# Three token mixers dealt over a projection stream: another order of the mixers' inputs and of emission

## The chip, the cores and the metric

The kernel runs on one core of a Trainium2 chip. The metric is the device time of one execution in microseconds (us); shown is the median of several runs. One execution is also profiled. Engines are named PE (matrix), DVE (vector), ACT (scalar), POOL (GpSimd) and SP (sync); PEld is PE's weight load.

## The reference

Two layers of a decoder trunk on 256 tokens of width 1024, in float32. In each layer:

```python
x = LN(a*x + 0.5*SwiGLU_1(x))                       # width 2816
h = x @ w_in                                        # split among three mixers and merge gates
x = LN(a*x + (sum_b sigmoid(h_gate_b) * (Mixer_b(h_b) @ w_branch_b)) @ w_o)
x = LN(a*x + 0.5*SwiGLU_2(x))
x = LN(a*x + sigmoid(x @ w_pg) * (p[i] @ w_pp))
```

The mixers are causal and independent of each other: branch 0 is RWKV-7 (8 heads of 64), branch 1 is gated linear attention, GLA (4 heads, keys 64, values 128), branch 2 is Gated DeltaNet (4 heads of 128, a convolution over 4 tokens ahead of it). RWKV and DeltaNet both need the inverse of a unit triangular matrix for each chunk. Each mixer is a chain: small products on PE, each followed by work on ACT or DVE that the next product waits for.

## The kernel before

All weights come from memory as blocks of 128 x 1024 (`raw`). ACT rounds a block to a short format (`hi`), DVE subtracts (`lo`), and each product of activations with weights is three matmuls (high with high, high with low, low with high) of 256 or 512 columns. The feed-forward parts (`h`, `y`, `tb`) run as a steady stream of such matmuls. Four `raw` and four `hi`/`lo` buffers turn over, loaded by SP in the order in which `plan()` lists the blocks.

The mixer part of a layer has four generators:

- S, `stream`: the columns of `w_in`, one block of 256 columns at a time (PE writes `cb`), in the order of `MIX`. First come two fixed blocks (`wa`; `misc`, which has the small inputs of all three mixers, and `ab`, DeltaNet's gates). Then the items of `MIX`: `C_R`, `C_K`, `C_V` are RWKV's inputs (tile `c`, one shift step on DVE per 128 columns), `C_DQ`, `C_DK`, `C_DV` DeltaNet's (tile `c`, a convolution of three DVE steps per 128 columns), `C_LQ` GLA's queries and keys (`lqk`), `C_LV` its values (`st`). A pair such as `(2, 0)` is half of the merge gate of branch 2: `cb` is copied to `sg` and sent to memory (`gd`) until it is needed (`sgate`). `("w", b, h)` is the product of the finished branch b with half h of `w_branch` (`pj`), into the merge `mg`.
- R, `rwkv`: `pw`; normed keys (`kk`, `sq`); operands spread to `ls` and `bk`; grams (PE `gram`, DVE masks into `gram` and `ls`, ACT copies); transposes `bkt`; the inverse (`rig`, `rigt`, `riab` on DVE, then `rix`, `rih`, `ric`); `vm`, `bon`; four chunks (`rp`, `ru`, `ry`, `rd`), and per half of the tokens an output (`rv`, `pg`, `ro`).
- D, `gdn`: gates (`x`, `gcol`, `grow`, `dd`), norms (`un`), `pk`, `pq`, its inverse (`gig` to `gih`), `gtt` to `gto`, `ktr`, two chunks (`gv`, `gd`, `go`).
- L, `gla`: `gk`, a scan (`lxb`), seven levels (DVE and ACT make `lw`, PE `lg`, DVE writes `latt` under a mask), `lc`, `lo`.

D's first step makes `x` from `ab` in some 20 small steps on DVE with an exponential on ACT between them, and its second step starts with `gcol` and `grow`.

`mixers` steps through the letters of `ORDER`; a letter advances its generator to its next bare `yield`. A generator that yields a name waits for an input, and then the stream (or the maker of that name) is stepped until it is there:

```python
def step(self, name):
    for need in self.threads[name]:
        if need is None:
            return
        while need not in self.got:
            self.step(self.maker.get(need, "S"))
    self.over.add(name)
```

So code is emitted in this order. The build then sets each engine's queue from it with a list scheduler of its own, which may move instructions that are not pinned to program order. On the chip every engine takes its queue in order: an instruction that waits holds all behind it.

`plan()` and `merge` follow `MIX` as well: the last item's half decides which half of `w_o` comes last.

Of the kernel before, what the change touches and what calls it, by code (L numbers as in the profile page):

```python
# [44 lines left out]
C_R, C_K, C_V, C_WA, C_GLO = 0, 512, 1024, 1536, 1664  # L45
C_LQ, C_LK, C_LV, C_LGK, C_LG = 1824, 2080, 2336, 2848, 2864
C_DQ, C_DK, C_DV, C_DAB, C_DG = 3376, 3888, 4400, 4912, 4920
# [4 lines left out]
B_LG, B_DG, B_ALOG, B_DT, NB = 0, 128, 256, 260, 264  # L52
K_ID, K_ONES64, K_M0, K_M1, K_M16, K_OFF16, K_INCL, K_HP, K_HF, K_CENT, NK = (
    0, 128, 256, 384, 512, 544, 672, 800, 802, 804, 932)
MIX = (C_R, C_K, C_DK, C_LV, (0, 0), C_V, C_LQ, (0, 1), C_DQ, (2, 0), (1, 1), C_DV, (2, 1), (1, 0), ("w", 0, 0),
       ("w", 1, 1), ("w", 0, 1), ("w", 1, 0), ("w", 2, 0), ("w", 2, 1))
ORDER = ("RRSRSSSDSSRSRRSSSRRRRRRRRRRSSRSRRRSDRRRRRSRSRDRRRRRRRRDRDSDRLDRRDRDLRDDSDSSSLDLDRLRDRRRDRDDRRRDLRLDD"
         "SDDDDSDLLSDDDLLRDLSDLLRRLLDSSDSDSLLSSSSDSLDS")
LEVELS = (64, 32, 16, 8, 4, 2, 1)


# [5 lines left out]
def plan():  # L67
# [13 lines left out]
    for i in range(DEPTH):  # L81
# [4 lines left out]
        out.append(("fmisc", i))  # L86
        for item in MIX:
            if isinstance(item, tuple) and item[0] == "w":
# [5 lines left out]
            else:  # L94
                out.extend(("fcol", i, item + 256 * u) for u in range(2))
        last = MIX[-1][2]
        out.extend(("wo", i, h, u) for u in (1 - last, last) for h in range(2))
# [137 lines left out]
class Trunk:  # L235
# [434 lines left out]
    def mixers(self, i):  # L670
# [3 lines left out]
        self.threads = {"S": self.stream(i), "R": self.rwkv(i), "D": self.gdn(i), "L": self.gla(i)}  # L674
        for name in ORDER + "RDLS":
            self.step(name)
# [4 lines left out]
    def stream(self, i):  # L681
# [26 lines left out]
        yield  # L708
        for item in MIX:
            if isinstance(item, tuple) and item[0] == "w":  # L710
                yield "b%d" % item[1]
                self.project(i, *item[1:])
                if item != MIX[-1]:
                    yield
# [949 lines left out]
```

## Time and profile before

| what | us |
|---|---|
| median of 3 runs (1572.3 to 1577.93) | 1574.76 |
| the profiled execution, its own time | 1568.71 |
| span of its instructions | 1566.9 |
| PE busy | 1494.9 (95%) |
| PEld busy | 1356.7 (87%) |
| DVE busy | 1058.5 (68%) |
| ACT busy | 873.3 (56%) |
| mean granted clock of PE | 0.981 |

The mixer parts run from about 227 to 545 us and from about 1007 to 1325 us of the span. A busy PE is not PE at its peak, since matmuls overlap in the records. Matmul groups in float32 without the split appear twice as often in the trace as in the program's queue.

### The profile page before, as it was taken

What the parts mean: (1) busy time and instruction counts of PE and PEld (TensorE: products, weight loads), DVE (VectorE), ACT (ScalarE), POOL (GpSimd) and SP (SyncE); (2) the same over time, 40 slices, a digit from 0 to 9 for tenths busy, and PEclk for the clock granted to TensorE, in tenths of its full rate; (3) what the DMA queues carried; (4) which work ended last, traced back from release to release, by engine and by line L of the source; (5) the groups of instructions that cost most, each with busy time, mean ns of one, the idle gap of its engine ahead of it and who ended that gap; (6) DMA issues with size and microseconds to landing.
All of it is one profiled execution on the core that took longest, in us unless ns stands there. A gap on an engine that the chain in (4) does not pass through costs nothing. (4 is left out here: it accounts for less than half of the span.)

```text
span 1566.9 us, 27601 instructions
## 1 busy us (share of the span) xinstructions
PE 1494.9 (95%) x11280; PEld 1356.7 (87%) x11280; DVE 1058.5 (68%) x1597; ACT 873.3 (56%) x1229; POOL 49.1 (3%) x85
## 2 busy tenths in 40 slices
PE   8999999988998999999999999998989889999997
PEld 7999889887987989998789997897979879899986
DVE  5555757787975875556865557577789658745567
ACT  5544558856654554445654445587665555644453
POOL 0000000000002000000000000000000020000001
PEclk9999999989999999999999999999999999999999
DMA  7765655532424655656555666554425256656562
GB/s 257 264 215 189 216 190 161 169 127 80 151 84 168 233 184 177 223 189 216 177 180 192 216 189 194 195 170 153 136 75 156 82 200 219 188 170 222 189 217 81
DMA packets 79775, 277.96 MB, mean 177 GB/s; under 512 B 9376, under 2 KB 9760, under 8 KB 79648
## 3 DMA queue, kind: packets, MB, share of 16 engines
q1 hardware_dynamic: 75744, 262.76, 51.8%
q0 software_dynamic: 3616, 13.11, 2.2%
q8 instruction: 88, 1.44, 0.4%
q10 hardware_dynamic: 288, 0.33, 0.1%
q14 instruction: 39, 0.32, 0.1%
HBM read 264.63 MB, written 11.53 MB: 176 GB/s over the span
## 5 line engine op out<-in xcount | busy, mean ns | idle before, releaser
L223 DVE TENSOR_TENSOR lo<-raw,hi 128x1024 fp32r<-128x1024 f32 (+1 forms) x459 | 555.4, 1220 | 316.1 <-ACT hi L223 313.7
L223 ACT CAST hi<-raw 128x1024 fp32r<-128x1024 f32 (+1 forms) x459 | 474.9, 1047 | 430.1 <-PE h L223 144.1
L223 PE MATMUL h<-xh,hi 128*128 128x256 f32 x1088 | 306.2, 282 | 5.9 <-ACT hi L223 5.5
L223 PE MATMUL h<-xl,hi 128*128 128x256 f32 x1088 | 305.8, 281 | 0.8 <-DVE xl L223 0.8
L223 PE MATMUL h<-xh,lo 128*128 128x256 f32 x1088 | 305.4, 281 | 0.0
L223 PE MATMUL cb<-xh,hi 128*128 128x256 f32 x864 | 247.1, 286 | 14.4 <-DVE c L223 11.1
L223 PE MATMUL cb<-xl,hi 128*128 128x256 f32 x864 | 244.5, 283 | 0.0
L223 PE MATMUL cb<-xh,lo 128*128 128x256 f32 x864 | 243.4, 282 | 0.0
L223 PEld LDWEIGHTS h<-xh,hi 128*128 128x128 f32 x1088 | 204.9, 189 | 7.3 <-ACT hi L223 5.5
L223 PEld LDWEIGHTS h<-xh,lo 128*128 128x128 f32 x1088 | 208.6, 192 | 0.1
L223 PEld LDWEIGHTS h<-xl,hi 128*128 128x128 f32 x1088 | 205.1, 189 | 2.2 <-DVE xl L223 1.0
L223 PEld LDWEIGHTS cb<-xh,hi 128*128 128x128 f32 x864 | 164.7, 191 | 18.8 <-DVE c L223 11.3
L223 PEld LDWEIGHTS cb<-xl,hi 128*128 128x128 f32 x864 | 164.8, 191 | 2.4 <-issue 1.0
L223 PEld LDWEIGHTS cb<-xh,lo 128*128 128x128 f32 x864 | 164.7, 191 | 1.9 <-issue 1.0
L223 PE MATMUL y<-hi,gh 128*128 128x512 f32 x352 | 137.8, 391 | 0.0
L223 PE MATMUL y<-lo,gh 128*128 128x512 f32 x352 | 137.1, 389 | 0.0
L223 PE MATMUL y<-hi,gl 128*128 128x512 f32 x352 | 136.2, 390 | 0.3 <-DVE gl L223 0.3
L223 PE MATMUL tb<-hi,xl 128*128 128x512 f32 x224 | 87.6, 391 | 2.1 <-DVE xl L223 2.1
L223 PE MATMUL tb<-hi,xh 128*128 128x512 f32 x224 | 88.5, 395 | 0.0
L223 PE MATMUL tb<-lo,xh 128*128 128x512 f32 x224 | 88.0, 393 | 0.0
L223 PEld LDWEIGHTS y<-hi,gl 128*128 128x128 f32 x352 | 66.1, 188 | 14.7 <-DVE gl L223 0.8
L223 PEld LDWEIGHTS y<-lo,gh 128*128 128x128 f32 x352 | 66.1, 188 | 12.2
(354 smaller groups left out, 2264.0 us busy)
## 6 DMA issues: line engine op xcount, KB each, us to landing
raw<-in_ws_dram SPq DMA_DIRECT2D x457, 512.0 KB, 4.4
gb<-in_ln_dram SPq DMA_DIRECT2D x16, 512.0 KB, 6.1
gd<-sg SPq DMA_DIRECT2D x32, 256.0 KB, 4.2
sgate<-gd POOLq DMA_DIRECT2D x12, 512.0 KB, 5.8
xd<-x POOLq DMA_DIRECT2D x4, 512.0 KB, 5.8
x<-xd POOLq DMA_DIRECT2D x4, 512.0 KB, 9.0
sw<-in_sw_dram SPq DMA_DIRECT2D x2, 768.0 KB, 8.7
xt<-in_xt_dram SPq DMA_DIRECT2D x4, 256.0 KB, 5.4
```

The source lines that it names most:

```text
L223: ins = f(*args, **kw)
```

## The change

Two tables get other values. `MIX` sets the order of the stream's blocks: RWKV's keys come first, then its receptance, and gates of branch 2 and GLA's queries move up; the `pj` products, last in both, run branch 1, 2, 0 in place of 0 and 1 mixed, then 2. `ORDER` deals the steps of R, D and L in a nearly regular pattern between the steps of S. No operation is added or removed.

```diff
-MIX = (C_R, C_K, C_DK, C_LV, (0, 0), C_V, C_LQ, (0, 1), C_DQ, (2, 0), (1, 1), C_DV, (2, 1), (1, 0), ("w", 0, 0),
-       ("w", 1, 1), ("w", 0, 1), ("w", 1, 0), ("w", 2, 0), ("w", 2, 1))
-ORDER = ("RRSRSSSDSSRSRRSSSRRRRRRRRRRSSRSRRRSDRRRRRSRSRDRRRRRRRRDRDSDRLDRRDRDLRDDSDSSSLDLDRLRDRRRDRDDRRRDLRLDD"
+MIX = (C_K, C_R, (2, 0), C_LQ, C_V, C_DK, C_DQ, (2, 1), C_LV, (1, 0), C_DV, (1, 1), (0, 0), (0, 1),
+       ("w", 1, 0), ("w", 1, 1), ("w", 2, 0), ("w", 2, 1), ("w", 0, 0), ("w", 0, 1))
+ORDER = ("SRRSRDDSLSSRRSRRSRRSRRSRRSRRSRLRSRLRSRLRSRLRSRLRSRLRSRLRSRDLRDSRDLRDSRDLRDSRDLRDSRDLRDDSRDLRDDSR"
...
```

What it does to the queues, at three places of the first layer. First, PE's queue around `gcol`, the product that starts DeltaNet's second step. Before, it stood behind RWKV's last gram:

```order
L223 MATMUL gram<-ls_2960,bk_2964 128x128
L223 MATMUL gram<-ls_2962,bk_2964 128x128
L223 MATMUL bkt<-kc,bk_2964 128x128 x4
L223 MATMUL gcol<-x,kc 128x8
L223 MATMUL cb<-xh,hi 128x256
L223 MATMUL cb<-xl,hi 128x256
L223 MATMUL cb<-xh,lo 128x256
```

Now it stands right behind the last `misc` and the two `ab`, with `grow` and GLA's `gk` next and 107 `cb` behind them:

```order
L223 MATMUL misc<-xh,hi 128x256
L223 MATMUL misc<-xl,hi 128x256
L223 MATMUL misc<-xh,lo 128x256
L223 MATMUL ab<-kc,mx 128x8 x2
L223 MATMUL gcol<-x,kc 128x8
L223 MATMUL grow<-kc,x 128x128 x8
L223 MATMUL gk<-gl_2286,sw 128x256 x2
L223 MATMUL cb<-xh,hi 128x256
```

So `gcol` and `grow` moved up past some 440 matmuls of the stream and RWKV's grams. Second, DVE's queue among the masks of RWKV's grams, ahead of its inverse. Before, the masks and `rig` follow each other with few steps of other chains:

```order
L223 TENSOR_TENSOR ls_2962<-gram,kc 64x512
L223 SCALAR_TENSOR_TENSOR c_3145<-cb,cv,c_3145 128x255 x2
L223 TENSOR_TENSOR gram_2986<-gram,kc 64x4x64
L223 TENSOR_TENSOR ls_2960<-gram,kc 64x512
L223 TENSOR_TENSOR rig<-gram_2986,kc 32x32x8 x2
L223 TENSOR_TENSOR gram_2986<-gram,kc 64x4x64
L223 TENSOR_TENSOR ls_2962<-gram,kc 64x512
L223 TENSOR_TENSOR rig<-gram_2986,kc 32x32x8 x2
L223 COPY gcol<-gcol 128x8
L223 SCALAR_TENSOR_TENSOR c_3145<-cb,cv,c_3145 128x255 x2
L223 STREAM_TRANSPOSE rigt<-rig 128x512
```

Now GLA's levels stand between them:

```order
L223 TENSOR_TENSOR ls_2724<-gram,kc 64x512
L223 COPY lw<-lxb 128x4x64
L223 TENSOR_TENSOR lw<-lxb 128x4x64
L223 TENSOR_TENSOR lw<-lxb 128x8x32 x2
L223 SCALAR_TENSOR_TENSOR c_3093<-cb,cv,c_3093 128x255
L223 TENSOR_TENSOR lo<-raw,hi 128x1024 x2
L223 SCALAR_TENSOR_TENSOR c_3093<-cb,cv,c_3093 128x255
L223 TENSOR_TENSOR lw<-lw,lqk 128x4x64 x2
L223 TENSOR_TENSOR lw<-lw,lqk 128x8x32 x2
L223 TENSOR_TENSOR gram_2940<-gram,kc 64x4x64
L223 TENSOR_TENSOR ls_2722<-gram,kc 64x512
L223 TENSOR_TENSOR rig<-gram_2940,kc 32x32x8 x2
```

The levels of GLA (`lw`, `latt`) moved from the second half of the mixer part into RWKV's grams and inverse, and the convolution of DeltaNet's keys with them. Third, PE's queue at the end, behind RWKV's last `rv`. Before, the last part of GLA's output and the first products on branch 0 came next (`bh` is the high part of a finished branch, `tp` a transpose):

```order
L223 MATMUL lo<-lv,lcross 128x128
L223 MATMUL lo<-lv,latt 128x128
L223 MATMUL pj_5398<-bh,hi 128x256
L223 MATMUL pj_5424<-bh,hi 128x256
L223 MATMUL tp<-kc,mo 128x128 x8
L223 MATMUL pj_5398<-bl,hi 128x256
```

Now all of `cb` is done by then, and 288 `pj` follow in one run, of which the first 192 are on branches 1 and 2:

```order
L223 MATMUL ry<-gram_2940,uz 64x64 x2
L223 MATMUL pg<-gl_2286,sw 128x128 x8
L223 MATMUL rv<-rsq,kc 128x512
L223 MATMUL pj_5426<-bh,hi 128x256
L223 MATMUL pj_5426<-bl,hi 128x256
L223 MATMUL pj_5426<-bh,lo 128x256
```

So the products that need RWKV's result moved behind 192 that don't.

More of the change, by code (lines that the diff above doesn't have):

```diff
@@ L54 @@
     0, 128, 256, 384, 512, 544, 672, 800, 802, 804, 932)
-MIX = (C_R, C_K, C_DK, C_LV, (0, 0), C_V, C_LQ, (0, 1), C_DQ, (2, 0), (1, 1), C_DV, (2, 1), (1, 0), ("w", 0, 0),
-       ("w", 1, 1), ("w", 0, 1), ("w", 1, 0), ("w", 2, 0), ("w", 2, 1))
-ORDER = ("RRSRSSSDSSRSRRSSSRRRRRRRRRRSSRSRRRSDRRRRRSRSRDRRRRRRRRDRDSDRLDRRDRDLRDDSDSSSLDLDRLRDRRRDRDDRRRDLRLDD"
-         "SDDDDSDLLSDDDLLRDLSDLLRRLLDSSDSDSLLSSSSDSLDS")
+MIX = (C_K, C_R, (2, 0), C_LQ, C_V, C_DK, C_DQ, (2, 1), C_LV, (1, 0), C_DV, (1, 1), (0, 0), (0, 1),
+       ("w", 1, 0), ("w", 1, 1), ("w", 2, 0), ("w", 2, 1), ("w", 0, 0), ("w", 0, 1))
+ORDER = ("SRRSRDDSLSSRRSRRSRRSRRSRRSRRSRLRSRLRSRLRSRLRSRLRSRLRSRLRSRDLRDSRDLRDSRDLRDSRDLRDSRDLRDDSRDLRDDSR"
+         "DLRDDSRDLRDDSRDLRDDSRDLRDDSRDLRDDSRDRDDSRRSRSSSSS")
 LEVELS = (64, 32, 16, 8, 4, 2, 1)
```

## The prediction

> **What bounds the kernel now.** I read the windows view first, over the stretch of each layer from the first `pw` (the first chain matmul) to the `wo` matmuls: columns are span, busy time of PE, PEld, DVE, ACT, POOL, then granted clock, DMA share, GB/s.
>
> ```profile
> 227.00:545.00 318.00, 294.93 (x2789) 271.92 (x2788) 243.76 (x437) 205.66 (x301) 13.58 (x25) 0.95 0.45 146
> 1007.00:1325.00 318.00, 294.00 (x2791) 270.56 (x2789) 243.94 (x438) 206.83 (x302) 12.72 (x23) 0.96 0.45 146
> 300.00:320.00 20.00, 12.64 (x106) 10.98 (x105) 19.59 (x35) 8.70 (x18) 0.00 (x0) 0.81 0.32 105
> ```
>
> PE is the bound of the stage (295 of 318 us), DVE follows at 77%. The third row is the one to keep: in 300 to 320 DVE is full (19.59 of 20) and PE is what waits (12.64). So DVE's total leaves room over the stage, but not in every part of it. Then the groups of instructions on PE, for both layers together; behind the second bar stand the idle time ahead of the group and what ended it.
>
> ```profile
> L223 PE MATMUL pj<-bh,hi 128*128 128x256 f32 x192 | 56.0, 294 | 12.0 <-ACT bh L223 12.0
> L223 PE MATMUL cb<-xh,hi 128*128 128x256 f32 x864 | 247.1, 286 | 14.4 <-DVE c L223 11.1 <-ACT hi L223 1.9 <-ACT sg L223 1.4
> L223 PE MATMUL un<-usq,eps 128*128 128x512 f32 x16 | 11.8, 853 | 8.0 <-ACT usq L223 8.0
> L223 PE MATMUL gram<-ls,bk 64*128 64x128 f32 x128 | 13.1, 291 | 1.6 <-ACT bk L223 1.1 <-ACT bkt L223 0.5
> L223 PE MATMUL bkt<-kc,bk 128*128 128x128 f32 x32 | 5.2, 286 | 2.5 <-DVE ls L223 2.5
> L223 PE MATMUL gcol<-x,kc 128*128 128x8 f32 x4 | 1.0, 318 | 0.8 <-DVE ls L223 0.8
> L223 PE MATMUL lg<-lw 64*128 64x64 f32 x224 | 18.2, 279 | 0.5 <-DVE gic L223 0.5
> L223 PE MATMUL rix<-rit,riof 128*64 128x64 f32 x128 | 4.2, 224 | 0.0
> ```
>
> The reader is to see where PE stands still today: at `pj` for branch 0 (12.0), at a `cb` block whose PSUM bank DVE's convolution steps had not yet read (11.1), at `un` (8.0), and around the grams (1.6, 2.5, 0.8). That is 36.0 us in two layers, 18.0 a layer.
>
> **The change part by part.** No matmul, vector or scalar operation is added or taken away; only places in the queues change. So each term is a wait that goes or a wait that comes.
>
> *What goes.* In the new order 192 `pj` matmuls on branches 1 and 2 stand between RWKV's last `rv` and the first `pj` on branch 0. Matmuls of this shape follow each other every 0.11 us:
>
> ```profile
> 225.25 0.28 PE L223 MATMUL cb<-xh,hi 128*128 128x256 f32 x1
> 225.37 0.28 PE L223 MATMUL cb<-xl,hi 128*128 128x256 f32 x1
> ```
>
> 192 of them give some 22 us of cover for a wait that was 6.0: it goes. `un` is now dealt between `lg` and `rih` matmuls and goes too; the `cb`, `gram`, `bkt` and `gcol` waits lie in the stretch that term B prices anew, so I take the old ones off whole: -18.0 a layer, at best. If `un` and the grams keep theirs it is -11.5.
>
> *Term A, the gates of the delta rule.* In the queue of PE, `gcol` now stands directly behind `misc` and `ab`; before, it stood behind the last `gram`. PE can't pass it. Its price is the chain from `misc` to `gcol`'s operand `x`, which ran before beside other work, here ACT's and DVE's rows in order of time (start, duration):
>
> ```profile
> 241.04 0.28 PE L223 MATMUL misc<-xh,lo 128*128 128x256 f32 x1
> ...
> 242.85 0.47 ACT L223 ACTIVATE mx<-misc,om 128x256 f32<-128x256 f32 x1
> 243.70 1.28 ACT L223 ACT_TABLE_LOAD   x1
> 245.00 0.42 ACT L223 ACTIVATE gl<-mx 32x256 f32<-32x256 f32 x1
> 245.43 0.41 ACT L223 COPY gl<-mx 16x256 f32<-16x256 f32 x1
> 248.13 0.16 ACT L223 COPY ab<-ab 128x8 f32<-128x8 f32 x1
> 250.22 1.28 ACT L223 ACT_TABLE_LOAD   x1
> 251.51 0.21 ACT L223 ACTIVATE e<-e 128x8 f32<-128x8 f32 x1
> ...
> 244.12 0.47 DVE L223 SCALAR_TENSOR_TENSOR mx<-misc,cv,mx 128x255 f32<-128x255 f32 x1
> 249.61 0.15 DVE L223 TENSOR_TENSOR x<-ab,br 128x8 f32<-128x8 f32 x1
> 251.75 0.17 DVE L223 TENSOR_SCALAR s<-e 128x8 f32<-128x8 f32 x1 [1.04 <-ACT e L223]
> 257.36 0.17 DVE L223 SCALAR_TENSOR_TENSOR x<-x,al 128x8 f32<-128x8 f32 x1
> ```
>
> From the end of `misc` (241.32) to the end of `mx` (244.59): 3.3. From there the chain's own work: `gl` twice 0.83, `ab` 0.16, four small steps on DVE about 0.6, a table load and `e` 1.5, then some 15 steps of 0.17 us each, 2.6: 5.7. Behind `gcol` come `grow` and `gk`, and the next `cb` needs a bank that ACT and DVE free only after the eight `dd` of `grow` and the product of `dd`:
>
> ```profile
> L223 ACT ACTIVATE dd<-grow,gcol 128x128 f32<-128x128 f32 x16 | 4.3, 390 | 0.0
> L223 ACT ACTIVATE dd<-dd 128x1024 f32<-128x1024 f32 x2 | 2.3, 1130 | 0.0
> ```
>
> Eight at 0.27 are 2.2, two copies of a `cb` bank near 0.5 each 1.0, `dd` on ACT 1.1, its product on DVE about the same, a step 0.5: near 6, of which PE works 1.5 on `grow` and `gk`: 4.5. A = 3.3 + 5.7 + 4.5 = 13.5 a layer. Bounds: 9, if `mx` comes at once; 20, if other work stands in between as it did before (244.59 to 257.53 is 12.9 in place of 5.7). It is nearest to the lower kind of row, since little of other work stands in DVE's queue there. Before, PE waited nothing for these matmuls.
>
> The price of a table load is worth a look. The trace has `gl` starting at 245.00, 0.02 behind the end of the load. The Trainium skill (ScalarE: Activation LUTs, What ACT_TABLE_LOAD costs) adds a drain of about 1.38 us to each switch; by it three switches would make A about 4 longer and the forecast about 8 later. The row shows no such gap, so I leave it out.
>
> *Term B, DVE's queue between the first `gram` and the solve of RWKV's inverse.* The new order has most of GLA's levels (`lw`, `latt`) and the convolution of DeltaNet's keys and part of its queries in this stretch; before, neither was there. Counted from the first `gram` to the `rih` that waits for a `latt`, PE's queue has 256 `cb` (29.2 at 0.114), 32 `gram` (6.5 by half of 13.1), 16 `bkt` (2.6), 48 `lg` (7.8) and 32 `rix` (2.1): 48.2 us. DVE's queue in the same stretch has 144 instructions, by these rows:
>
> ```profile
> L223 DVE TENSOR_TENSOR lo<-raw,hi 128x1024 fp32r<-128x1024 f32 (+1 forms) x459 | 555.4, 1220 | 316.1 <-ACT hi L223 313.7 <-issue 0.3 <-PE cb L223 0.3
> L223 DVE SCALAR_TENSOR_TENSOR c<-cb,cv,c 128x255 f32<-128x255 f32 (+2 forms) x96 | 45.5, 477 | 5.0 <-ACT c L223 3.7
> L223 DVE COPY_PREDICATED latt<-masks,lg 128x256 f32<-128x256 uint8 (+1 forms) x32 | 15.8, 552 | 4.4 <-PE lg L223 4.4
> L223 DVE TENSOR_TENSOR lw<-lw,lqk 128x256 f32<-128x256 f32 x32 | 12.1, 420 | 0.2
> L223 DVE TENSOR_TENSOR lw<-lxb 128x256 f32<-128x256 f32 (+1 forms) x30 | 10.9, 408 | 0.0
> L223 DVE TENSOR_TENSOR ls<-gram,kc 64x512 f32<-64x512 f32 x16 | 11.0, 689 | 0.2
> L223 DVE TENSOR_TENSOR gram<-gram,kc 64x256 f32<-64x256 f32 x16 | 6.7, 417 | 0.1
> L223 DVE TENSOR_TENSOR rig<-gram,kc 32x256 f32<-32x256 f32 x16 | 9.4, 589 | 0.3
> L223 DVE TENSOR_TENSOR rigt<-riab 128x1 f32<-128x1 f32 (+14 forms) x30 | 9.2, 305 | 1.0
> L223 DVE TENSOR_REDUCE riab<-rigt 128x1 f32<-128x1 f32 (+14 forms) x30 | 7.1, 238 | 0.8
> L223 DVE TENSOR_TENSOR riof<-gram,kc 128x1024 f32<-128x1024 f32 x4 | 4.7, 1220 | 0.0
> L223 DVE STREAM_TRANSPOSE rigt<-rig 128x512 f32<-128x512 f32 x6 | 4.2, 704 | 3.2 <-ACT rit L223 3.2
> ```
>
> By busy time over count: 14 `lo` 16.9; 23 steps on `c` 10.9; 31 `lw` 11.5; 11 `latt` 5.4; 8 `ls` 5.5; 8 `gram` 3.4; 8 `rig` 4.7; 15 pairs of `rigt` and `riab` 8.2; two `riof` and three transposes 4.4; the rest, six small ones, 3.0: 73.9. Neighbours overlap by up to 0.08 (the timeline), so 71. In the queue of `before` the same chain has 87 instructions, about 53 us, beside PE's 52 (79 more `cb`): balanced, and yet full in 300 to 320. Now 71 stands against 48: PE has nothing to pass the waiting `lg`, `rih` and `cb` with, and loses 22.5. DVE also stands idle there while a matmul or an ACT copy comes; bounds 0 (always something else ready) and 9 (as much as PE lost around the grams and the `cb` behind them before, 36.0 - 12.0 - 8.0 over two layers, is 8). I take 6, nearer to that row, since the chain of RWKV is the same. B = 28.5.
>
> *What I price at nothing.* DMA: SP's queue moves only the gate writes among the `raw` loads, at a share of 0.45. Cover: four `raw` buffers. If it went, a `cb` would wait for `hi`. Delta's inverse now meets RWKV's last chunks (`gix`, `rd`, `gih` close together): between -2 and +5, taken as 0. The clock is a rival below.
>
> Sum a layer: 13.5 + 28.5 - 18.0 = +24, two layers +48. On the profiled execution (1568.7) that is 1616.7; the median of the three runs shown lies 6.1 above the profiled one, so 1622 or 1623.
>
> **The rivals.** *The interleaving works: faster.* The Trainium skill (Perfetto Trace Analysis, Optimization Strategy) says that where the most contended engine changes with the stage, interleaving the stages may help. Here it would mean that no new wait comes and the old 36 us go, with up to 28 us of clock (318 us at 0.95 and 0.96 lack 16 and 13): 1511 to 1539. For it speaks the tail (`pj`), against it the sum of DVE's queue; it decides if that sum is at most PE's 48 and `gcol` finds `x` ready. 0.06.
>
> *DVE catches up: slower, but by little.* A at 9, B at 20 without idle time: +11 a layer, 1597. The 0.08 overlaps and the masks that wait for nothing speak for it. 0.14.
>
> *The clock adds to it.* After each long wait the granted clock fell (0.81 in the third row). With waits in more places, PE may run slow in the parts where it alone is the bound (the 320 `cb` behind A, 36 us), 4 to 9 us a layer: 1630 to 1645. By the Trainium skill (TensorE: Matmul & The Clock Gate, Part 1) an idle window of about 3.4 us halves the clock until one busy window has passed, so each of A's waits could bring it; the trace's 0.81 agrees in kind. Against: in B a slow PE costs nothing, DVE being behind. 0.12.
>
> *New waits equal old ones.* If A came out at 5 and B at 13, as with `x` early and a third less work in DVE's stretch than I count, the time would stand at 1570 to 1580; no row speaks for it. 0.03.
>
> **How the numbers follow.** The likeliest, 0.65, is 1623 with its own 1603 to 1640 (A 9 to 18, B 22.5 to 31.5, not all at one end). A measurement of this kernel can tell about 0.3%, 5 us. Slower: 0.65 + 0.14 + 0.12 = 0.91; same 0.03; faster 0.06. The range takes in the second rival and the lower half of the third: 1593 to 1647 leaves out under 2 in 10.
>
> **What would show it.** A: in the new trace PE waits for DVE `mx` and `x` ahead of `ab` and `gcol`, 8 us or more together, and for `c` at the `cb` behind `gk`. B: a stretch of some 65 us early in the stage with DVE busy over nine tenths and PE below seven, and waits of 3 to 5 us at `lg` for `lw` or `latt`. The tail: no wait of `pj` for `bh`. The forecast is wrong if DVE shows idle time in that stretch while PE is busy, if PE passes `ab` and `gcol` within 3 us, or if new waits of over 5 us come in the second half, where I have none.

## The result, and the profile after

| | us |
|---|---|
| after, median of 4 runs (1623.3 to 1633.62) | 1627.82 |
| before, median of 4 runs (1572.3 to 1577.93) | 1574.63 |
| ratio, 95% interval | 1.0338 [1.0297, 1.0379] |
| the profiled execution after, its own time and span | 1630.34, 1628.6 |
| mean granted clock, before and after | 0.981, 0.963 |

The change costs 53 us; the forecast was 1623 with a range of 1593 to 1647. The two profiled executions lie 61.6 apart, since the one of before lies below its median and the one of after above.

The windows view after, both layers from the first `pw` to the `wo` matmuls, then the first layer from the first `gram` to the `rih` that waits for a `latt`, and 20 us in it (span, then PE, PEld, DVE, ACT, POOL, clock, DMA share, GB/s):

```profile
227.00:575.00 348.00, 309.14 (x2808) 285.84 (x2807) 244.60 (x438) 206.48 (x301) 13.09 (x26) 0.92 0.40 134
1039.00:1385.00 346.00, 307.29 (x2804) 283.41 (x2802) 245.81 (x440) 208.50 (x303) 11.80 (x21) 0.92 0.41 135
...
307.20:380.60 73.40, 57.24 (x497) 53.48 (x496) 64.97 (x143) 38.01 (x60) 0.92 (x3) 0.82 0.26 87
...
325.00:345.00 20.00, 14.88 (x115) 14.43 (x116) 18.76 (x52) 5.15 (x9) 0.00 (x0) 0.74 0.23 78
```

The stage that took 318 us takes 348 and 346, with the same DVE work (244 to 246 us) and a lower clock (0.92 for 0.95). The third row is the stretch of term B: DVE's 143 instructions are busy for 65.0 of 73.4 us, PE for 57.2. The fourth is 20 us out of it.

The groups of PE after, in both layers (busy, mean ns, behind the bar idle time ahead of the group and what ended it):

```profile
L223 PE MATMUL pj<-bh,hi 128*128 128x256 f32 x192 | 55.1, 287 | 0.0
L223 PE MATMUL un<-usq,eps 128*128 128x512 f32 x16 | 9.0, 644 | 0.0
L223 PE MATMUL gram<-ls,bk 64*128 64x128 f32 x128 | 13.1, 291 | 0.0
L223 PE MATMUL bkt<-kc,bk 128*128 128x128 f32 x32 | 5.2, 287 | 0.0
L223 PE MATMUL cb<-xh,hi 128*128 128x256 f32 x864 | 256.2, 297 | 20.1 <-DVE c L223 12.6 <-ACT lqk L223 5.8 <-ACT hi L223 1.6
L223 PE MATMUL lg<-lw 64*128 64x64 f32 x224 | 26.3, 337 | 23.2 <-DVE latt L223 17.0 <-DVE lw L223 6.2
L223 PE MATMUL gcol<-x,kc 128*128 128x8 f32 x4 | 1.2, 372 | 10.7 <-DVE x L223 10.7
L223 PE MATMUL ab<-kc,mx 8*128 8x8 f32 x4 | 0.7, 238 | 6.3 <-DVE mx L223 6.3
L223 PE MATMUL gk<-gl,sw 128*128 128x256 f32 x8 | 3.6, 546 | 4.1 <-ACT lxb L223 4.1
L223 PE MATMUL gih<-gitt,giof 128*64 128x64 f32 x64 | 3.1, 271 | 4.3 <-ACT gitt L223 4.3
L223 PE MATMUL gix<-git,giof 128*64 128x64 f32 x64 | 2.3, 225 | 4.2 <-ACT git L223 4.2
```

The waits of `pj`, `un`, `gram` and `bkt` are gone. In their place stand `ab`, `gcol` and `gk` (21.1 in two layers), `lg` (23.2), `cb` for `c` and for `lqk` (18.4, before 11.1 and none worth a row), and `gih` and `gix` of the delta rule's inverse (8.5).

Term A in the timeline of the first layer (start, duration, in brackets the idle time ahead):

```profile
246.24 0.38 PE L223 MATMUL ab<-kc,mx 8*128 8x8 f32 x2 [3.16 <-DVE mx L223]
251.95 0.60 PE L223 MATMUL gcol<-x,kc 128*128 128x8 f32 x2 [5.33 <-DVE x L223]
252.40 3.48 PE L223 MATMUL grow<-kc,x 128*128 128x128 f32 x16
258.74 1.12 PE L223 MATMUL gk<-gl,sw 128*128 128x256 f32 x2 [2.15 <-ACT lxb L223]
...
244.44 0.47 ACT L223 ACTIVATE mx<-misc,om 128x256 f32<-128x256 f32 x1
244.93 1.28 ACT L223 ACT_TABLE_LOAD   x1
246.22 0.41 ACT L223 ACTIVATE gl<-mx 32x256 f32<-32x256 f32 x1
```

From the end of `misc` (246.24 - 3.16 = 243.08) to `gcol` (251.95) it took 8.9 us; the sum of the chain was 9.0. The three last rows are the table load and its neighbours on ACT: it starts 0.02 behind `mx`, and what follows starts 0.01 behind its end. The Trainium skill (ScalarE: Activation LUTs, What ACT_TABLE_LOAD costs) adds about 1.38 us of drain to each switch; this trace shows it on neither side of the load.

### The profile page after: what moved, and what is told of

The parts are those of the page before. It is cut to its first block, busy times and chain, and to the rows that moved or that the text cites. A ratio compares the mean times of both kernels' runs of the same rounds, so it can differ in the third digit from the quotient of the medians.

```text
span 1628.6 us, 27620 instructions
## 1 busy us (share of the span) xinstructions
PE 1521.8 (93%) x11280; PEld 1382.0 (85%) x11280; DVE 1060.0 (65%) x1597; ACT 872.8 (54%) x1227; POOL 49.9 (3%) x85
## 5 line engine op out<-in xcount | busy, mean ns | idle before, releaser
L223 PE MATMUL cb<-xh,hi 128*128 128x256 f32 x864 | 256.2, 297 | 20.1 <-DVE c L223 12.6
L223 PE MATMUL cb<-xh,lo 128*128 128x256 f32 x864 | 252.7, 293 | 0.4 <-DVE lo L223 0.4
L223 PE MATMUL cb<-xl,hi 128*128 128x256 f32 x864 | 252.0, 292 | 0.0
L223 PEld LDWEIGHTS cb<-xh,hi 128*128 128x128 f32 x864 | 172.5, 200 | 27.2 <-DVE c L223 12.8
L223 PEld LDWEIGHTS cb<-xl,hi 128*128 128x128 f32 x864 | 172.8, 200 | 2.6 <-issue 1.4
L223 PEld LDWEIGHTS cb<-xh,lo 128*128 128x128 f32 x864 | 171.6, 199 | 3.5 <-issue 1.9
L223 PEld LDWEIGHTS y<-hi,gl 128*128 128x128 f32 x352 | 66.1, 188 | 13.9
```

The source lines that it names most:

```text
L223: ins = f(*args, **kw)
```

## Experiments

**The gates alone.** One letter of `ORDER` is moved, the second `D`:

```diff
-ORDER = ("SRRSRDDSLSSRRSRRSRRSRRSRRSRRSRLRSR...
+ORDER = ("SRRSRDSLSSRRSRRSRRSRRSRRSRRSRDLRSR...
```

> The changed kernel, with the delta rule's second step (gcol, grow, dd) emitted behind RWKV's last gram in place of behind its first step; all else as changed. Theory (term A is a price of its own: PE stands still for the gates' chain and nothing later takes that time in): the waits at ab, gcol and gk and at the cb behind them go, some 13.5 us a layer, and the stretch of the grams keeps its own price. 1627.8 - 27 = 1601 us, 1595 to 1606; ratio to the kernel before 1.013 to 1.020. Rival (DVE is so late at the grams that PE merely arrives there earlier and waits longer): the waits move to lg and cb in the grams' stretch, 1620 to 1628, ratio above 1.028.

Measured 1587.06 us, ratio 1.0089 [1.0061, 1.0117]: 40.8 us below the changed kernel, more than the theory's 27. The windows view of the 35 us behind `misc`, of before, of the changed kernel and of this one:

```profile
240.00:275.00 35.00, 35.00 (x251) 32.09 (x250) 26.24 (x52) 30.57 (x45) 0.00 (x0) 1.00 0.54 171
```

```profile
240.00:275.00 35.00, 22.88 (x150) 21.27 (x149) 17.50 (x40) 23.93 (x44) 0.00 (x0) 0.76 0.23 73
```

```profile
240.00:275.00 35.00, 34.16 (x277) 32.44 (x276) 24.80 (x49) 34.31 (x53) 0.00 (x0) 1.00 0.51 154
```

PE is full again (34.2 of 35, before 22.9), and the clock that had fallen to 0.76 is back at 1.00. With `gcol` far behind, the list scheduler also puts `ab`, `gk` and `grow` apart, each between `cb` matmuls. In the groups of this kernel these four wait for nothing:

```profile
L223 PE MATMUL grow<-kc,x 128*128 128x128 f32 x32 | 4.5, 274 | 0.0
L223 PE MATMUL gk<-gl,sw 128*128 128x256 f32 x8 | 2.4, 377 | 0.0
L223 PE MATMUL gcol<-x,kc 128*128 128x8 f32 x4 | 0.6, 216 | 0.0
L223 PE MATMUL ab<-kc,mx 8*128 8x8 f32 x4 | 0.6, 213 | 0.0
...
L223 PE MATMUL lg<-lw 64*128 64x64 f32 x224 | 32.2, 351 | 21.5 <-DVE latt L223 13.8 <-DVE lw L223 6.4 <-ACT c L223 1.3
```

The rival (the wait only moves on to the grams) is out: `lg` waits 21.5 for the 23.2 of before this edit, no more. From the first `pw` to the first `gram`, with nearly the same queue on PE, this kernel needs 58.8 us in the first layer and 58.6 in the second, the changed one 75.4 and 74.7: A is 16.6 and 16.1. In the first layer 11.8 of that is idle time of PE and 4.8 slower matmuls (PE busy for 60.2 of 75.4 us, now for 55.4 of 58.8). The other 8 us of the 40.8 lie elsewhere, most of them behind the first `gram`.

**The gates early in the old order.** The other way round, in the kernel before:

```diff
-ORDER = ("RRSRSSSDSSRSRRSSSRRRRRRRRRRSSRSRRRSDRRRRRSR...
+ORDER = ("RRSRSDDSSSSRSRRSSSRRRRRRRRRRSSRSRRRSRRRRRSR...
```

> The kernel before, with the first two steps of the delta rule emitted right behind misc, and nothing else moved; in PE's queue gcol then stands 114 cb (13 us) behind the last misc, ahead of the grams, and not right behind ab as in the changed kernel. Theory (A is the chain from misc to gcol and the way through dd behind it): the 9.0 us of chain have 13 us of cover here if nothing else stands in DVE's queue, so gcol waits 0 to 5 us, and the cb behind grow waits the 4.5 to 6 us of dd: +4.5 to +11 us a layer, 1584 to 1597, ratio 1.006 to 1.014. Rival (the place of the gates costs nothing by itself; only the new order as a whole does): 1572 to 1578.

Measured 1602.63 us, ratio 1.0181 [1.0164, 1.0198]: +28, above the theory's 9 to 22 and far from the rival's nothing. The waits from the first `pw` to behind the grams, first layer (us in all, times, longest):

```profile
PE cb L223 <- DVE c L223: 11.3, 2, 6.2
PE gcol L223 <- DVE x L223: 3.0, 1, 3.0
PE bkt L223 <- DVE ls L223: 2.4, 1, 2.4
```

`gcol` waits 3.0 and the `cb` behind `grow` 5.0 (the other 6.2 are those that stood at 5.5 before): 8.0 a layer, inside the expected 4.5 to 11. What was missed is the rest of the 14 a layer: waits at the grams grow by 1 to 2 us, and the mean clock falls from 0.981 to 0.974.

**Does the clock fall because PE waits?** Products that nothing reads fill two of the waits, the first line ahead of `ab`, the last ahead of `gcol`:

```diff
+        self.fill(ps, 6)
...
+    def fill(self, ps, n):
+        self.hold = True
+        for _ in range(n):
+            self.mm(ps[:, 256:], self.ident, self.sw[:, :256])
+        self.hold = False
...
+        self.fill(pg, 10)
```

> The changed kernel with idle products in two of term A's waits: 6 matmuls of 128 x 256 in float32 ahead of ab and 10 ahead of gcol, on constants, into columns of the same banks that nothing reads; about 0.5 us each by gk's place in the trace, so 3.1 and 5.2 us where PE stood still 3.2 and 5.3. Nothing else moves. Theory (the stretches at half clock behind these waits come from PE standing still): the stretches of 10.2 and 6.8 us at half clock behind them shorten or go, and of the 21 us that PE is late at the first gram 4 to 6 go: 1616 to 1621 us, ratio 1.026 to 1.030. Rival (the clock falls for another reason): 1626 to 1632.

Measured 1616.27 us, ratio 1.0263 [1.0244, 1.0283]: 11.5 us faster than the changed kernel with 16 matmuls a layer more. The timeline of this kernel, then two windows of it, then the first window in the changed one:

```profile
240.72 2.75 PE L223 MATMUL ab<-sw,kc 128*128 128x256 f32 x12
244.04 0.29 PE L223 MATMUL ab<-kc,mx 8*128 8x8 f32 x2 [0.57 <-DVE mx L223]
244.25 4.58 PE L223 MATMUL gcol<-sw,kc 128*128 128x256 f32 x20
249.75 0.39 PE L223 MATMUL gcol<-x,kc 128*128 128x8 f32 x2 [0.92 <-DVE x L223]
250.00 2.03 PE L223 MATMUL grow<-kc,x 128*128 128x128 f32 x16
...
255.07 0.70 PE L223 MATMUL gk<-gl,sw 128*128 128x256 f32 x2 [1.81 <-ACT lxb L223]
257.67 0.58 PE L223 MATMUL cb<-xh,hi 128*128 128x256 f32 x1 [1.90 <-DVE c L223]
```

```profile
245.00:255.00 10.00, 6.81 (x38) 5.42 (x36) 4.19 (x23) 5.44 (x18) 0.00 (x0) 1.00 0.14 48
257.00:263.00 6.00, 5.33 (x25) 5.34 (x26) 3.24 (x7) 2.69 (x4) 0.00 (x0) 0.50 0.00 0
```

```profile
245.00:255.00 10.00, 3.43 (x16) 3.33 (x17) 4.44 (x22) 4.28 (x9) 0.00 (x0) 0.51 0.31 110
```

`gcol` starts 9.0 us behind the first filling matmul (249.75 - 240.72), as late as ever; but the ten us in which the changed kernel had the clock at 0.51 now have 1.00, and the eight `grow` take 2.03 in place of 3.48. That the clock fell there because PE stood still is shown. The rule of the Trainium skill (TensorE: Matmul & The Clock Gate, Part 1) that an idle window of some 3.4 us halves the clock agrees in kind; in the changed kernel half clock began within the first wait, of 3.16 us: from 245.3 to 246.2 us the clock is 0.50, from 244 to 245 still 1.00.

The second stretch that was named, of 6.8 us, did not go: from 257 to 263 us the clock is 0.50, at waits of only 1.81 and 1.90 us. Nor need there be a long wait: in the kernel with the gates late the clock is 0.50 from 322 to 338 us, with PE busy for 14.7 of these 16 us and no wait over 1.5 us since 312; why is open. And the time did not come where it was meant to. From the first `pw` to the first `gram` this kernel needs 72.3 and 72.4 us, 3.1 and 2.3 less than the changed one, where 4 to 6 a layer were expected; the rest of the 11.5 us came elsewhere, where the edit touches nothing. That the total fits the theory is in part luck.

**The levels alone.** GLA's steps from the second on stand one behind each of RWKV's steps, from the 33rd of its 56 on:

```diff
-...SRRSRRSRLRSRLRSRLRSRLRSRLRSRLRSRLRSRDLRDSRDLRDSRDLRDS...
+...SRRSRRSRRSRRSRRSRRSRRSRRSRRSRRSRDRDSRDRLDSRLDRLDSRLDR...
```

> The changed kernel, with GLA's levels (lw, lg, latt) and what follows them emitted from the end of RWKV's inverse on, one step for each step of RWKV, in place of from its beginning on, one for two. Theory (term B is the sum of DVE's queue): 31 lw and 11 latt, 16.9 us by the same rows, leave a stretch that loses 7.8 us of lg on PE, so its price falls by 8 to 9 us a layer; later the levels stand between work with more room on DVE and bring back 0 to 4: 1610 to 1620 us, ratio 1.023 to 1.029. Rival 1 (given back whole, the levels wait as long wherever they stand): 1625 to 1632. Rival 2 (the stretch's price is RWKV's own chain from engine to engine and not the sum): the waits at rih and cb grow by as much as those at lg go, 1625 to 1630.

Measured 1610.04 us, ratio 1.0237 [1.0213, 1.0261]: 17.8 us faster, the most that the theory gave. The way there was another than expected. The groups of PE in this kernel:

```profile
L223 PE MATMUL cb<-xh,hi 128*128 128x256 f32 x864 | 252.3, 292 | 24.7 <-DVE riab L223 10.7 <-DVE c L223 6.1 <-ACT lqk L223 5.5
...
L223 PE MATMUL lg<-lw 64*128 64x64 f32 x224 | 20.2, 288 | 5.7 <-DVE latt L223 5.7
...
L223 PE MATMUL rih<-ritt,riof 128*64 128x64 f32 x128 | 8.0, 310 | 5.3 <-ACT riof L223 5.2
L223 PE MATMUL pk<-c 128*128 128x128 f32 x32 | 6.8, 338 | 4.4 <-DVE c L223 4.4
```

`lg` waits 17.5 less and `cb` for `c` 6.5 less, but `cb` for `riab`, `rih` (0.9 in the changed kernel) and `pk` wait 19.5 more: counted in these waits alone, rival 2 is nearly right. In the sum of all waits the edit brought `gix` and `gih`, which no longer wait (8.5), and the clock. The stretch of term B itself can be compared, since but for `lg` PE has the same products in it; from the first `gram` to the first `rih`, in this kernel:

```profile
305.40:357.10 51.70, 42.93 (x401) 40.28 (x400) 47.85 (x93) 29.48 (x47) 1.79 (x5) 0.93 0.35 114
```

It lasts 51.7 us, in the changed kernel 73.4, with DVE busy for 47.9 in place of 65.0. Less the 7.8 us of `lg`, B fell by 13.9 in the first layer, more than the 8 to 9 expected, which speaks against rival 2; behind it the levels take part of that back (from the last `rih` to `wo` 160 us in place of 148). PE lost work there too, so the next run takes work from DVE alone.

**Less work on DVE.** Two of three convolution steps are left out, which frees nothing but DVE:

```diff
-        for s in range(1, 4):
+        for s in range(1, 2):
```

> The changed kernel without two of the three shifted steps of DeltaNet's convolution: 24 instructions of 0.47 us a layer fewer on DVE, some 13 of them in the stretch from the first gram to RWKV's rih; PE and ACT keep all their work. Theory (term B is the sum of DVE's queue): the stretch gets cheaper by what DVE no longer does there, about 6 us a layer, and up to 2 more behind it: 1611 to 1617 us, ratio 1.023 to 1.027. Rival (DVE is full there but PE waits for chains through ACT and PE as well): less than 2 us a layer, 1624 to 1628.

Measured 1601.14 us, ratio 1.0172 [1.0147, 1.0197]: -26.7, where the theory had -11 to -17. In the groups of this kernel `lg` lost the whole wait for `latt`:

```profile
L223 PE MATMUL lg<-lw 64*128 64x64 f32 x224 | 20.3, 308 | 11.2 <-DVE lw L223 8.4 <-ACT c L223 2.8
...
L223 DVE SCALAR_TENSOR_TENSOR c<-cb,cv,c 128x255 f32<-128x255 f32 x48 | 22.7, 479 | 9.3 <-ACT c L223 9.1
```

Some 21 us less work on DVE (the changed kernel's `c` steps are busy for 43.4 us) made the kernel 26.7 faster, though DVE is idle for about 100 us a layer over the stage (348 - 245). From the first `gram` to the last `rih` this kernel needs 107.8 and 105.5 us, the changed one 114.5 and 113.8: 6.7 and 8.3 a layer, where the theory said 6 and the rival under 2. The rival is out. The excess lies mostly behind the stretch (3.5 a layer up to `wo`), the rest ahead of it and outside the mixers, and was not followed.

**Both late.**

> The changed kernel with both: the delta rule's second step behind the last gram and GLA's levels from the end of RWKV's inverse on. Alone they gave -40.8 and -17.8 us. Theory (two separate queues' prices that add): 1627.8 - 58.6 = 1569 us, 1565 to 1576; the tail without the wait of pj then stays as the gain of the change, so this may end up to 0.6% below the kernel before. Rival (the two overlap: both free the same DVE time ahead of rih): 1575 to 1587, no better than the gates alone.

Measured 1578.38 us, ratio 1.002 [1.0001, 1.004]: 9 us short of the sum, outside the theory's 1565 to 1576 and inside the rival's range, though 9 us better than the gates alone, which the rival did not have. Windows and waits of this kernel show where part of it went:

```profile
296.00:316.00 20.00, 18.70 (x168) 17.41 (x165) 19.00 (x38) 13.29 (x29) 0.00 (x0) 1.00 0.33 107
316.00:336.00 20.00, 12.95 (x97) 12.78 (x96) 19.52 (x46) 9.59 (x13) 0.00 (x0) 0.83 0.37 108
```

```profile
PE cb L223 <- DVE riab L223: 14.1, 2, 7.0
```

Without the levels DVE is still full for 40 us (19.0 and 19.5 of 20), now with the convolution of DeltaNet's keys among RWKV's masks, and the 7.0 us at one `cb` are what the levels alone had shown as 5.3. PE reaches this place 16 us earlier and waits longer. That is 3.4 of the 9 us (14.1 for 10.7); the rest has no place. Whether the changed `MIX` has a price of its own was not tried: no run has it with the old `ORDER`.

**The tail.** The order of the branch products alone, new in the old kernel and old in the new one:

```diff
-       ("w", 0, 0), ("w", 1, 1), ("w", 0, 1), ("w", 1, 0), ("w", 2, 0), ("w", 2, 1))
+       ("w", 1, 0), ("w", 1, 1), ("w", 2, 0), ("w", 2, 1), ("w", 0, 0), ("w", 0, 1))
```

> The kernel before, with only the order of the branch products changed to that of the changed kernel: branch 1, 2, 0 (pj). Theory 1 (as predicted: 192 pj on other branches cover the wait for bh of branch 0): -6 us a layer, 1560 to 1566, ratio 0.990 to 0.995. Theory 2 (the letters decide: in the old order DeltaNet and GLA finish their outputs as late as RWKV, so the first pj now waits for another branch's output): 1572 to 1578, ratio 0.998 to 1.002.

> The changed kernel, with only the order of the branch products set back: branch 0 first, then 0 and 1 mixed, then 2 (pj). Theory (the 192 pj on branches 1 and 2 are the cover): pj waits 6 us for bh again in each layer, +12, 1636 to 1644, ratio to the kernel before 1.039 to 1.044. Rival (the new letters alone bring RWKV's output in time): 1625 to 1630.

In the old kernel it gives nothing, as theory 2 had it: 1578.64 us, ratio 1.0014 [0.9999, 1.0028]. The wait only changes its name, from `pj` for `bh` (12.0 in both layers) to the transposes of DeltaNet's and GLA's output:

```profile
L223 PE MATMUL pj<-bh,hi 128*128 128x256 f32 x192 | 54.6, 290 | 1.3 <-ACT bh L223 1.3
...
L223 PE MATMUL tp<-kc,mo 128*128 128x128 f32 x32 | 6.9, 360 | 11.8 <-DVE mo L223 11.8
```

In the new kernel, set back, it costs 24 us (1652.14, ratio 1.0488 [1.0466, 1.051]), twice what was expected: the wait of `pj` is there (12.3 in two layers), and with it the mean clock falls from 0.963 to 0.957. From the last `rih` to `wo` it is 8.1 and 9.0 us longer; the rest lies elsewhere and has no explanation. So the gain in the tail is of order and letters together: the 192 `pj` are a cover only where branches 1 and 2 are finished early.

**An order that beats both.** The first experiments say what an order must keep apart. Starting from the kernel before, single letters were moved and neighbours of `MIX` exchanged where, with the durations of its trace, an instruction at the head of PE's queue then waits less:

```diff
-MIX = (C_R, C_K, C_DK, C_LV, (0, 0), C_V, C_LQ, (0, 1), C_DQ, ...
+MIX = (C_R, C_K, C_DK, C_LV, C_V, (0, 0), (0, 1), C_LQ, C_DQ, ...
+ORDER = ("RRSRSSSDRSSRSRSSRSRRRRRRRRRSSRSRRRSDRRRRRSRSRDRRRRRRRRDRDSDRRLDRRRDDLDDSDSSSLDLRLDRDRRRDRDDDRRRD"
+         "LRLDDSDDDSSDLLLDDDLSRRDLLDLRLLSSDDSLDLSSSSSDSLDS")
```

> The kernel before, with some fifteen letters of ORDER moved by a few places and three neighbours of MIX exchanged (C_V ahead of two gates, C_LQ behind them), chosen so that an instruction that waited in the trace of before stands later in its queue or what it waits for earlier; the branch products keep their order. What is meant to go, a layer: 5 of the 6.0 of pj for bh (branch 0's output comes some 5 us earlier against PE's queue), 1.9 of gtf, 1 of un's 4.0, 3 at and behind the grams; the wait of cb for c (5.5) stays, ahead of the grams now; the inverse of the delta rule gets 2 us of new waits. Theory (the price of an order is the sum of the waits at its single places): -8 to -9 us a layer, 1575 - 17 = 1558 us, 1553 to 1565, ratio 0.986 to 0.994. Rival (waits taken away at one place come back at others, as in old_tail_new): 1570 to 1580.

Measured 1553.99 us, ratio 0.9865 [0.9843, 0.9888], 4 us below the theory's 1558 and inside its range. The clock of the execution and the wait of `pj` in the first layer, then this layer from the first `pw` to `wo`, in this kernel and in the one before:

```profile
core 0: 1551.3 us, clock 0.992
```

```profile
PE pj L223 <- ACT bh L223: 2.7, 2, 2.0
```

```profile
230.10:526.70 296.60, 279.21 (x2740) 258.10 (x2739) 237.02 (x430) 201.25 (x295) 13.55 (x25) 0.99 0.46 150
```

```profile
229.70:539.50 309.80, 286.73 (x2741) 264.68 (x2740) 238.85 (x430) 201.93 (x295) 13.58 (x25) 0.95 0.45 145
```

`pj` waits 2.7 a layer in place of 6.0, `gtf` 0.4 for 1.9, and the clock rises from 0.981 to 0.992. But the theory's sum is not how the time came. The first layer's 296.6 us with PE busy for 279.2, before 309.8 with 286.7, are 5.7 us less idle time, where 8 to 9 were meant to go, and 7.5 less busy time for the same matmuls. Over both layers about half of the gain is the faster clock, which the theory had left out; that the total came out is in part luck.

## Why the prediction was right, by its steps

The time (1628 for 1623) was right in sign and size. Step by step, a layer:

- *What goes* (-18.0): the waits of `pj`, `un`, `gram` and `bkt` are all gone, as the groups show. That the 192 `pj` cover the tail by themselves was too simple: in the old order they don't. The tail gave more than priced, since with the long waits gone its clock rose: from the last `rih` to `wo` of the first layer the granted clock is 0.98 over 147.6 us, before 0.94 over 172.3, so 3 us of clock are missing there in place of 10 (in the second layer 3 in place of 7).
- *Term A* (13.5, bounds 9 to 20): 16.6 and 16.1 by the gates moved alone. The chain was sized to 0.1 us (8.9 for 9.0); of what lies behind it 2.2 at `gk` and 1.5 at `cb` were seen, 3.7 for 4.5. What was missed is the clock behind the waits. The waits at `ab` and `gcol`, 8.5 together, and the one of `cb` behind `gk` are the signs that were named.
- *Term B* (28.5, own range 22.5 to 31.5): the stretch was to last 48.2 + 28.5 = 76.7 us and lasted 73.4 in the first layer. DVE was busy for 65.0, not 71, and stood idle for 8.4, not 6: B = 73.4 - 48.2 = 25.2. The mechanism stands (less DVE work there, less time), but only 16.2 of the 25.2 are idle time of PE; the other 9.0 are matmuls that took longer than their row (PE busy for 57.2, not 48.2), beside a clock of 0.82. One named sign of being wrong did show: DVE idle while PE is busy, for 7.5 of its 8.4 us, mostly in waits for copies on ACT. The picture "DVE over nine tenths, PE below seven" was too strong: 65.0 and 57.2 of 73.4 are 0.89 and 0.78, and in the 20 us shown 18.8 and 14.9 (of 20). Two readings were off: 71 less 48.2 is 22.8, not 22.5, and the kernel before was compared up to its last `rih` (79 more `cb`); up to the first it has 275 `cb`, and DVE is busy for 44.1 of 52.9 us, not 53.
- *Priced at nothing.* The delta rule's inverse beside RWKV's last chunks, taken as 0 with bounds of -2 and +5, costs 4.3 (`gih` and `gix`, 8.5 in two layers): the mis-sized term among the small ones, at the upper bound. `cb` for `lqk` (2.9) had no term at all.
- *The clock*, given as a rival with 0.12 (1623 and twice 4 to 9 end at 1641, not at 1645), is not a rival but a part of the other terms: filling A's waits brought 5.4 us up to the first `gram` in both layers and 11.5 over the execution. Missing clock over the stage is 0.08 of 348 or 28 us, before 0.05 of 318 or 16. It was left out on the ground that a slow PE costs nothing where DVE is behind. That may hold in B, where no run tells whether the 9.0 us above cost anything; at A, where PE alone is the bound behind the wait, it does not.

So the forecast met the time in part because its omissions had opposite signs. A layer: 24 forecast, + 2.9 for A, + 2.9 for `lqk`, + 4.3 for the inverse, - 3.3 for B, - 6 for the tail's clock (7 and 4 in the two layers) make 25; 26.6 were measured (below), and some 2 us have no place of their own. That the forecast came within 5 us of the median is to that extent luck.

From the first `pw` to `wo` the two layers cost 27.7 and 25.5 us more than before, 53.2 in all. The other 8.5 of the 61.7 between the two profiled spans lie in the feed-forward parts (2 to 3.5 us in each of three), and in the longest of them no wait differs by more than 1 us. They are hardly a price of the change: these parts take 948 us in the profiled execution of before, and 953 to 958 in those of all ten other kernels, the fastest order among them. The execution of before that was profiled is rather a fast one (1568.71, below every timed run of it), and the two medians lie 53.2 apart.

## What to carry to other kernels

An instruction put early in an in-order queue must have its operand's whole chain covered by what stands ahead of it; add up that chain from the trace, and add what PE loses at half clock behind the wait, which here also came with two waits under 2 us. Dealing chains evenly by their total time on an engine says nothing about a stretch: count each engine's queue between two waits, since 65 us of DVE work beside 48 of PE's made a stretch of 73 even though DVE is free for over a quarter of the stage. And a wait removed at one place is a gain only if the next late thing on that queue is not as late: change the order of products and the letters that finish them together.

## What was not expected of the hardware

Filling two waits with 16 idle matmuls a layer made the kernel 11.5 us faster: from 245 to 255 us, around waits of 3.2 and 5.3 us, the changed kernel had half the clock, and the eight `grow` behind them took 3.48 us for 2.03. Half clock also came at waits of 1.81 and 1.90 us. Waits of PE thus cost more than their length: moving one letter was worth 40.8 us, and in the profiled executions PE's idle time fell by 33.3 (from 1628.6 - 1521.8 to 1586.7 - 1513.2) and its busy time, for the same matmuls, by 8.6.
